# Interleaving the blocks of full and small experts, one by one, in a two-layer diffusion backbone

## The chip, the cores and the metric

The kernel runs on one core of one Trainium2 chip. The metric is the device time in microseconds (us) of one execution of the whole program. Times of single parts come from one profiled execution, read as a page and as a trace.

## What is computed

Two layers of a latent generator over 256 latent and 256 context tokens of width 1024, in float32. Each layer has a mixer (gated linear attention, differential attention, neighbourhood attention) and a channel mixer. The channel mixer of layer 0 is a dense SwiGLU; that of layer 1, which reads only the 256 latent tokens, is a mixture of 8 experts of width 3584, two of them per token:

```python
def swiglu(h, wg, wu, wd):
    return (jax.nn.silu(h @ wg) * (h @ wu)) @ wd

def moe_swiglu(h, w_router, wg, wu, wd):
    t = h.reshape(-1, shp[-1])
    logits = (t @ w_router).astype(jnp.float32)
    top_v, top_i = lax.top_k(logits, TOP_K)
    top_w = jax.nn.softmax(top_v, axis=-1)
    gates = jnp.sum(jax.nn.one_hot(top_i, N_EXPERTS, dtype=jnp.float32) * top_w[..., None], axis=1)
    y = jnp.zeros_like(t)
    for e in range(N_EXPERTS):
        y = y + gates[:, e:e + 1].astype(t.dtype) * swiglu(t, wg[e], wu[e], wd[e])
```

The result is x plus the gated mixture, and one last RMSNorm. The change touches only this expert stage.

## The kernel before

Layer 0 and the mixer of layer 1 fill the first half of the program. Then comes the expert stage, from line 886 on. The kernel routes the tokens, sorts the experts by how many tokens they got (`order_experts`, `order_index`, L988 to L1029), and reads the sorted order into SyncE's registers (`load_order`, L1033), since the weights of expert number e in that order are fetched from an address that the registers give. Expert 0 is taken first whatever its load. The first four are **full** experts with room for 128 tokens, the last four **small** ones with room for 64. Tokens beyond that go through a loop at the end (L1378), which runs only if there are any.

Each expert is worked in 7 **blocks** of 512 of its 3584 inner columns. A block of either kind has three weight matrices, gate, up and down, and each of them comes in two loads of 1 MB (128 partitions x 2048 float32), so a block has 6 loads and an expert 42. All are issued by SyncE's queue in the order of the program.

- A full block (`expert`, L1172): `gate_up` (L1099) for gate and for up, 24 matmuls of 128x512 each, Silu and product (`act_mul`, L1108), transposition and split of the product (`g_T`, L1114), `down` (L1127), 24 matmuls more. Weights are split into a rounded part and a rest, so that three fast matmuls make one precise product: ScalarE writes the rounded part `eh` (L790), VectorE the rest `el` (L791), from the loaded tile `e`. There are three pairs of `eh` and `el`. The down projection of a block follows in the next block, after its gate and up.
- A small block (`expert_small`, L1221): weights are used as they are loaded, in plain float32, with two matmuls of 64 rows side by side: 32 matmuls for gate and up (L1254), 16 for down (L1242).

Loaded tiles live in a ring of named slots of 1 MB (L895 to L904). `first` gives the slots of the first 13 loads; after that the ring turns, and a slot drops out for good at the load number in `until`, when its memory is wanted for something else: ten slots at first, five from load 62 on. A slot is free again when its load has been converted (full) or multiplied (small).

The order of the experts is full 0 to 3, then small 4 to 7, and each expert's last down projection and its scatter into the output (`tail`) are done inside the next expert's first block. Work that is needed once is hooked behind chosen blocks by the table `plan`, whose keys are (expert, block):

```python
plan = {(0, 1): [order_experts], (0, 2): [order_index, lambda: onehots(1, 1, posp)], (0, 4): [lambda: gather_at(1, 1, x01, P), load_order],
        (0, 6): [lambda: row_bc(ga2b, lambda k: modT[1][:, 40 + k, 0:1])],
        (1, 1): [lambda: onehots(2, 2, posp)], (1, 4): [gather_pair],
        (2, 3): [add_x], (2, 5): [stack_ga2],
        (3, 1): [onehots_twice], (3, 4): [gather_rest],
        (4, 3): [lambda: row_bc(gfb, lambda k: gfT[:, k:k + 1])]}
```

`gather_at` brings one expert's tokens together by matmuls (L1078), `gather_pair` those of experts 2 and 3 at once, `gather_rest` those of the four small experts (L1094). PSUM has eight banks: four for gate and up (`pgu`, two tiles of two buffers), two for the down sums (`pdn`), two for everything else (`pmt`).

Of the kernel before, what the change touches and what calls it, by code (L numbers as in the profile page):

```python
# [20 lines left out]
P = 128  # L21
# [68 lines left out]
def hybrid_backbone_kernel(  # L90
# [674 lines left out]
    n_load = [0]  # L765

# [124 lines left out]
    pgu = pool("pgu", 2, space=PSUM)  # L891
# [12 lines left out]
    until = {"xc": 36, "xt": 42, "y": 42, "xh": 62, "xl": 62}  # L904
# [27 lines left out]
    for q in range(2):  # L932
        for t in range(2):
            pt = pgu.tile([P, 512], F32, tag="pg" if t == 0 else "pu", name="pht")
# [128 lines left out]
    def load_e(dram, kk, n):  # L1063
        i = n_load[0]
        n_load[0] += 1
        wh, wl = ready[i] if i in ready else convert(i, slot32(i), dram, kk, n, (mpr, mpr, mpc)[i % 3])
        return wh.rearrange("p (k n) -> p k n", n=n), wl.rearrange("p (k n) -> p k n", n=n)
# [19 lines left out]
    def gather_small():  # L1087
        n = (NE - NBIG) * (P // 2)
        xs = mp.tile([P, KD, n], F32, tag="xeH1", name="xs")
# [18 lines left out]
    def act_mul(pg, pu):  # L1108
        g = mp2.tile([P, 512], F32, tag="eg", name="eg", bufs=2)
        act(g, pg, AF.Silu)  # L1110
        tt(g, g, pu, ALU.mult)
        return g
# [59 lines left out]
    def expert(xe, wg, wu, wd, Sf, gate_col, tail, hooks=None, first=False, end=None):  # L1172
        pds = None
        prev = None
        for j in range(NJ):
# [14 lines left out]
            for f in (hooks or {}).get(j, ()):  # L1190
                f()
# [5 lines left out]
        def t1():  # L1197
            if end:
                tc.keep_in_program_order(nc.scalar.preload_act_table_set(LN_EXP))
                sc = scatter_pre(Sf, gate_col)  # L1200
                new_xg()
                for o in range(2):
                    down_cols(wd, last[0], pds, o)
                    scatter_half(sc, pds, o)
                    end(o)
                return
# [4 lines left out]
        return t0, t1  # L1211

# [8 lines left out]
    def expert_small(xs, wg, wu, wd, e, tail, hooks, end=None):  # L1221
# [4 lines left out]
        def g_Ts(g):  # L1226
# [3 lines left out]
            gt = mp2.tile([P, 4, H], F32, tag="gth", name="gts", bufs=2)  # L1230
# [15 lines left out]
        for j in range(NJ):  # L1246
            ps = pgu.tile([P, 512], F32, tag=("pg", "pu")[j % 2], name="pgs")
# [13 lines left out]
            g = mp2.tile([P, 512], F32, tag="eg", name="eg", bufs=2)  # L1261
# [7 lines left out]
            for f in (hooks or {}).get(j, ()):  # L1269
                f()  # L1270
# [37 lines left out]
    def new_xg():  # L1308
        nonlocal xg
        xg = mp.tile([P, 2, D], F32, tag="xeH0", name="xg")  # L1310
# [31 lines left out]
    def gather_pair():  # L1342
        xes[2] = gather_at(2, 2, xe_tiles(0))

# [3 lines left out]
    def stack_ga2():  # L1348
        for o in range(2):
# [3 lines left out]
    plan = {(0, 1): [order_experts], (0, 2): [order_index, lambda: onehots(1, 1, posp)], (0, 4): [lambda: gather_at(1, 1, x01, P), load_order],  # L1353
            (0, 6): [lambda: row_bc(ga2b, lambda k: modT[1][:, 40 + k, 0:1])],
            (1, 1): [lambda: onehots(2, 2, posp)], (1, 4): [gather_pair],
            (2, 3): [add_x], (2, 5): [stack_ga2],
            (3, 1): [onehots_twice], (3, 4): [gather_rest],
            (4, 3): [lambda: row_bc(gfb, lambda k: gfT[:, k:k + 1])]}
    tail = None
    for e in range(NE):  # L1360
        if e == 0:
            ws = [w[0, 0] for w in (wm_g, wm_u, wm_d)]
        else:
            ws = [w[0, ds(which[e], 1)].rearrange("o a b -> (o a) b") for w in (wm_g, wm_u, wm_d)]
        hooks = {j: f for (ee, j), f in plan.items() if ee == e}
        if e >= NBIG:
            tail = expert_small(xes[NBIG], *ws, e, tail, hooks, square if e == NE - 1 else None)
            continue
        xe, h = (x01, e * P) if e < 2 else (xes[2], (e - 2) * P)
        xv = (xe[0][:, :, h:h + P], xe[1][:, :, h:h + P])  # L1370
        gt_ = gates if e == 0 else gatp
        tail = expert(xv, *ws, lambda t, e=e: S[:, t, e, :], lambda t, e=e, g=gt_: g[:, t, e:e + 1], tail, hooks, e == 0)
    tail[0]()
    tail[1]()
# [3 lines left out]
    with tc.If(cv > 0):  # L1378
# [5 lines left out]
        for blk in range(2):  # L1384
            with tc.For_i(0, NE, 1) as ei:
# [9 lines left out]
                for f in expert(xv, sq_(wm_g), sq_(wm_u), sq_(wm_d), lambda t: S2[:, t, :], lambda t: gc[:, t:t + 1], None):  # L1395
# [36 lines left out]
```

## Time and profile before

| what | value |
|---|---|
| median of 3 runs | 1984.89 us (1984.31 to 1988.7) |
| profiled execution: its own time | 1986.53 us |
| profiled execution: span from first to last instruction | 1984.7 us |
| TensorE (PE) busy | 1836.6 us, 93% |
| VectorE (DVE) busy | 979.5 us, 49% |
| ScalarE (ACT) busy | 758.6 us, 38% |
| bytes read from HBM | 477.48 MB, 241 GB/s over the span |
| mean granted TensorE clock | 0.979 |

The page cuts the span into 40 slices of 49.6 us; slices 21 to 40 are the expert stage. Busy shares are averages over stages with different limits, so each stage has to be looked at by itself. PE matmuls overlap in the pipeline, so a busy PE need not be at its peak, and the length of a matmul's row is longer than the distance from one start to the next.

### The profile page before, as it was taken

How to read it: one execution, taken by the hardware profiler on the slowest of the kernel's cores; microseconds unless marked ns; L12 is line 12 of the kernel's file. 1: busy time of each engine (PE TensorE's matmuls, PEld its weight loads, DVE VectorE, ACT ScalarE, POOL GpSimd, SP SyncE). 2: the span in 40 equal slices, each digit the busy share in tenths (PEclk: the TensorE clock that was granted, in tenths of full speed). 3: DMA queues.
4: the chain of work that ended last, by engine and by line, in shares of the span. 5: the costliest groups of instructions: out<-in, count | busy, mean ns of one | idle time of the engine just before them, and what ended most of it. 6: DMA issues, size and time to landing. Idle time of an engine off the chain costs nothing.

```text
span 1984.7 us, 23236 instructions
## 1 busy us (share of the span) xinstructions
PE 1836.6 (93%) x9168; PEld 1256.5 (63%) x9168; DVE 979.5 (49%) x1296; ACT 758.6 (38%) x967; POOL 45.2 (2%) x73
## 2 busy tenths in 40 slices
PE   7998999999999999899899999999999878787886
PEld 4865766778887878677687878888784222222221
DVE  5474554633333345655678888988984001010101
ACT  4424454422222234245566777767662000000001
POOL 1030000000000000200000000000000000000000
PEclk9999999999999999999989999999999998999998
DMA  9555242342344244543489789999998999999996
GB/s 326 184 168 140 80 137 87 124 131 70 101 131 156 78 127 153 153 129 128 152 294 359 260 295 341 336 355 361 351 343 289 395 390 365 394 381 394 389 389 243
DMA packets 287090, 480.13 MB, mean 242 GB/s; under 512 B 12207, under 2 KB 142637, under 8 KB 286973
## 3 DMA queue, kind: packets, MB, share of 16 engines
q1 hardware_dynamic: 283488, 474.32, 67.8%
q0 software_dynamic: 1232, 2.42, 1.0%
q10 hardware_dynamic: 2252, 1.83, 0.3%
q8 instruction: 74, 1.21, 0.3%
q14 instruction: 44, 0.35, 0.1%
HBM read 477.48 MB, written 1.05 MB: 241 GB/s over the span
## 4 chain that ended last, share of the span: by engine, by line
PE 75%; DMA 14%; DVE 7%; ACT 2%; issue 1%; POOL 0%; SPq 0%; DVEq 0%; ACTq 0%; POOLq 0%
DMA e<-in_w_moe_up_dram 12%; PE pd L1134 8%; PE pgs L1254 7%; PE pds L1242 3%; PE pu L150 3%; PE pg L149 3%; PE pu L151 3%; PE pu L149 3%; PE pg L150 3%; PE pg L151 2%; PE psg L149 2%; PE psg L151 2%; PE psg L150 2%; PE psu L149 2%; PE psu L151 2%; PE psu L150 2%
## 5 line engine op out<-in xcount | busy, mean ns | idle before, releaser
L791 DVE TENSOR_TENSOR el<-e,eh 128x2048 fp32r<-128x2048 f32 (+1 forms) x173 | 375.6, 2190 | 49.2 <-ACT eh L790 48.2
L790 ACT ACTIVATE eh<-e 128x2048 fp32r<-128x2048 f32 (+1 forms) x173 | 316.6, 1839 | 92.7 <-PE pd L1134 31.8
L1254 PE MATMUL pgs<-e,xs 128*64 128x512 f32 x896 | 249.1, 635 | 72.5 <-DMA e<-in_w_moe_up_dram 65.9
L1254 PEld LDWEIGHTS pgs<-e,xs 128*64 128x64 f32 x896 | 70.0, 143 | 237.0 <-DMA e<-in_w_moe_up_dram 107.1
L142 ACT ACTIVATE wh<-w 128x2048 fp32r<-128x2048 f32 (+2 forms) x70 | 125.4, 1791 | 199.5 <-issue 78.3
L143 DVE TENSOR_TENSOR wl<-w,wh 128x2048 fp32r<-128x2048 f32 (+2 forms) x70 | 149.6, 2138 | 96.4 <-ACT wh L142 96.4
L1263 DVE TENSOR_TENSOR eg<-eg,pgs 64x512 f32<-64x512 f32 x28 | 19.3, 690 | 360.1 <-ACT eg L1262 360.1
L1262 ACT ACTIVATE eg<-pgs 64x512 f32<-64x512 f32 x28 | 16.5, 590 | 376.8 <-PE pgs L1254 376.8
L1242 PE MATMUL pds<-e,gts 128*64 128x512 f32 x448 | 126.6, 599 | 0.0
L149 PE MATMUL pg<-eh,xeH 128*128 128x512 f32 x224 | 89.7, 400 | 0.6 <-ACT eh L790 0.6
L149 PE MATMUL psp<-hH,wh 128*128 128x512 f32 (+1 forms) x224 | 86.8, 391 | 3.0 <-ACT hH L274 2.9
L150 PE MATMUL pg<-el,xeH 128*128 128x512 f32 x224 | 89.4, 399 | 0.0
L149 PE MATMUL pu<-eh,xeH 128*128 128x512 f32 x224 | 89.0, 398 | 0.0
L150 PE MATMUL pu<-el,xeH 128*128 128x512 f32 x224 | 88.3, 394 | 0.7 <-DVE el L791 0.6
L149 PE MATMUL psq<-wh,hH 128*128 128x256 f32 x304 | 88.7, 292 | 0.0
L151 PE MATMUL pg<-eh,xeL 128*128 128x512 f32 x224 | 88.5, 395 | 0.0
L151 PE MATMUL psq<-wh,hL 128*128 128x256 f32 x304 | 88.0, 290 | 0.0
L151 PE MATMUL pu<-eh,xeL 128*128 128x512 f32 x224 | 87.7, 392 | 0.0
L150 PE MATMUL psq<-wl,hH 128*128 128x256 f32 x304 | 87.5, 288 | 0.0
L150 PE MATMUL psp<-hL,wh 128*128 128x512 f32 (+1 forms) x224 | 85.6, 382 | 0.0
L151 PE MATMUL psp<-hH,wl 128*128 128x512 f32 (+1 forms) x224 | 85.0, 380 | 0.0
L1134 PE MATMUL pd<-eh,gth 128*128 128x512 f32 x224 | 71.2, 399 | 2.7 <-ACT eh L790 2.5
(504 smaller groups left out, 3445.5 us busy)
## 6 DMA issues: line engine op xcount, KB each, us to landing
e<-in_w_moe_gate_dram SPq DMA_DIRECT2D x111, 1024.0 KB, 7.6
e<-in_w_moe_up_dram SPq DMA_DIRECT2D x111, 1024.0 KB, 7.7
e<-in_w_moe_down_dram SPq DMA_DIRECT2D x111, 1024.0 KB, 7.1
wmod<-in_w_mod_dram SPq DMA_DIRECT2D x96, 512.0 KB, 4.7
w<-in_w_in_dram SPq DMA_DIRECT2D x24, 1024.0 KB, 6.4
w<-in_w_ffn_gate_dram SPq DMA_DIRECT2D x11, 1024.0 KB, 5.7
w<-in_w_ffn_up_dram SPq DMA_DIRECT2D x11, 1024.0 KB, 5.2
w<-in_w_out_dram SPq DMA_DIRECT2D x8, 1024.0 KB, 5.5
```

The source lines that it names most:

```text
L142: act(wh[:, :m], w32[:, :m], AF.Copy)
L143: tt(wl[:, :m], w32[:, :m], f32(wh[:, :m]), ALU.subtract)
L149: mm(ps, lhsT=sh, rhs=mh, start=first, stop=False)
L150: mm(ps, lhsT=sh, rhs=ml, start=False, stop=False)
L151: mm(ps, lhsT=sl, rhs=mh, start=False, stop=last)
L790: act(h3[:, b], w[:, b], AF.Copy)
L791: tt(l3[:, b], w[:, b], f32(h3[:, b]), ALU.subtract)
L1134: mm(pds[o], lhsT=gt[sh][:, q, :], rhs=w[mh][:, k, o * 512:(o + 1) * 512], start=a and j == 0 and q == 0, stop=z and j == NJ - 1 and q == 3)
L1242: mm(pd[0][H * o:H * o + H, :], lhsT=gt[:, q, :], rhs=w[:, k, o * 512:(o + 1) * 512], start=j == 0 and q == 0, stop=j == NJ - 1 and q == 3 ...
L1254: mm(ps[H * o:H * o + H, :], lhsT=xv[:, kk, :], rhs=ws[o][:, k, :], start=kk == 0, stop=kk == KD - 1, skip_group_check=True)
L1262: act(g[0:H], ps[0:H], AF.Silu)
L1263: tt(g[0:H], g[0:H], ps[H:P], ALU.mult)
```

## The change

The two expert functions become generators that stop after each block (`yield`), and a new loop takes one block of the full experts and then one of the small ones, the small ones four blocks behind:

```diff
+    LAG = 4
...
+    def full_ones():
+        tail = None
+        for e in range(NBIG):
+            h = e % 2 * P
+            xv = (x01[0][:, :, h:h + P], x01[1][:, :, h:h + P])
+            gt_ = gates if e == 0 else gatp
+            tail = yield from expert(xv, *weights(e), lambda t, e=e: S[:, t, e, :], lambda t, e=e, g=gt_: g[:, t, e:e + 1], tail, e == 0)
+        tail[0]()
+        tail[1]()
+
+    def small_ones():
+        tail = None
+        for e in range(NBIG, NE):
+            tail = yield from expert_small(xes[NBIG], *weights(e), e, tail, square if e == NE - 1 else None)
+        tail[0]()
+        tail[1]()
+
+    after = {0: [order_experts], 1: [order_index], 2: [onehots_twice], 3: [gather_rest, load_order],
+             4: [lambda: row_bc(ga2b, lambda k: modT[1][:, 40 + k, 0:1]), lambda: onehots(1, 3, posp)],
+             5: [lambda: gather_at(1, 1, x01, P)],
+             8: [add_x], 9: [stack_ga2], 10: [lambda: gather_at(2, 1, x01, 0)], 17: [lambda: gather_at(3, 1, x01, P)],
+             16: [lambda: row_bc(gfb, lambda k: gfT[:, k:k + 1])]}
+    bigs, smalls = full_ones(), small_ones()
+    for i in range(NBIG * NJ + LAG):
+        next(bigs, None)
+        if i >= LAG:
+            next(smalls, None)
+        for f in after.get(i, ()):
+            f()
+    next(smalls, None)
     finish()
```

Blocks 0 to 3 of the full experts stand alone, then come 24 pairs of a full and a small block, then the last 4 small blocks alone. The hooks move with it: the small experts' tokens are gathered after full block 3, the order is read into the registers there too, and experts 2 and 3 are gathered one by one (blocks 10 and 17) into the places that experts 0 and 1 leave free, where they were gathered together.

Memory is shared out anew, so that both kinds can be open at once: gate and up get one PSUM bank each instead of two, the small experts one for gate and up and one for down; the products have one buffer per kind; the small experts' tokens take the slot `xh` and the output the other half. The ring keeps `xl` for good, and the drop-outs come earlier:

```diff
-    pgu = pool("pgu", 2, space=PSUM)
+    pgu = pool("pgu", 1, space=PSUM)
...
-    until = {"xc": 36, "xt": 42, "y": 42, "xh": 62, "xl": 62}
+    until = {"xc": 26, "xt": 42, "y": 42, "xh": 22}
...
-        wh, wl = ready[i] if i in ready else convert(i, slot32(i), dram, kk, n, (mpr, mpr, mpc)[i % 3])
+        n_conv[0] += 1
+        wh, wl = ready[i] if i in ready else convert(i, slot32(i), dram, kk, n, (mpr, mpr, mpc)[(n_conv[0] - 1) % 3])
...
-        g = mp2.tile([P, 512], F32, tag="eg", name="eg", bufs=2)
+        g = mp2.tile([P, 512], F32, tag="eg", name="eg")
...
-            ps = pgu.tile([P, 512], F32, tag=("pg", "pu")[j % 2], name="pgs")
+            ps = pgu.tile([P, 512], F32, tag="ps", name="pgs")
...
-                pd[0] = pdn.tile([P, 512], F32, tag=f"pd{e % 2}", name="pds")
+                pd[0] = pdn.tile([P, 512], F32, tag="pds", name="pds")
```

Lines of the changed kernel stand 1 or 2 below those of before (L784, the load of a full expert, becomes L785; L790 and L791 become L791 and L792).

Three places show how the instructions move. The first is **SyncE's queue**. Before, in the middle of the small experts, every load is one of a small block (`e32` is the ring's tile), and waits for PE to have freed the slot:

```order
L1218 DMA e32_12251<-in_w_moe_gate_dram 128x4x512 [waits DMAHW2_49,PE_49]
L1218 DMA e32_12253<-in_w_moe_up_dram 128x4x512 [waits DMAHW3_49,PE_49]
L1218 DMA e32_12270<-in_w_moe_gate_dram 128x4x512 [waits DMAHW4_49,PE_49]
L1218 DMA e32_12272<-in_w_moe_up_dram 128x4x512 [waits DMAHW5_49,PE_49]
L1218 DMA e32_12285<-in_w_moe_down_dram 128x2x1024 [waits DMAHW6_49,PE_49]
L1218 DMA e32_12291<-in_w_moe_down_dram 128x2x1024 [waits DMAHW7_49,PE_49]
```

In the changed kernel six loads of a full block (L785) and six of a small one (L1218) take turns:

```order
L785 DMA e32_9114<-in_w_moe_gate_dram 128x4x512 [waits DMAHW2_49,PE_49]
L785 DMA e32_9132<-in_w_moe_gate_dram 128x4x512 [waits DMAHW3_49,PE_49]
L785 DMA e32_9160<-in_w_moe_up_dram 128x4x512 [waits DMAHW4_49,PE_49]
L785 DMA e32_9178<-in_w_moe_up_dram 128x4x512 [waits DMAHW5_49,PE_49]
L785 DMA e32_9199<-in_w_moe_down_dram 128x2x1024 [waits DMAHW6_49,PE_49]
L785 DMA e32_9217<-in_w_moe_down_dram 128x2x1024 [waits DMAHW7_49,PE_49]
L1218 DMA e32_9268<-in_w_moe_gate_dram 128x4x512 [waits DMAHW0_49,DVE_49]
L1218 DMA e32_9270<-in_w_moe_up_dram 128x4x512 [waits DMAHW1_49,DVE_49]
L1218 DMA e32_9287<-in_w_moe_gate_dram 128x4x512 [waits DMAHW2_49,DVE_49]
L1218 DMA e32_9289<-in_w_moe_up_dram 128x4x512 [waits DMAHW3_49,DVE_49]
L1218 DMA e32_9302<-in_w_moe_down_dram 128x2x1024 [waits DMAHW4_49,DVE_49]
L1218 DMA e32_9308<-in_w_moe_down_dram 128x2x1024 [waits DMAHW5_49,DVE_49]
```

With six slots and six loads per block, a full load now waits for PE to have used the small load in its slot, and a small one for VectorE to have converted the full load.

The second place is **ScalarE**, in the middle of the full experts. Before, conversions (`eh`) of the next loads stand close behind one another, with only the Silu (`eg`) and the split of the transposed product (`gth`) between them:

```order
L790 ACTIVATE eh_9105<-e32_9104 128x2048 [waits DMAHW1_49,DVE_49,PE_49]
L790 ACTIVATE eh_9123<-e32_9122 128x2048 [waits DMAHW2_49,DVE_49,PE_49]
L790 ACTIVATE eh_9151<-e32_9150 128x2048 [waits DMAHW3_49,DVE_49,PE_49]
L790 ACTIVATE eh_9169<-e32_9168 128x2048 [waits DMAHW4_49,DVE_49,PE_49]
L1161 ACTIVATE yHL_9080<-xT_70 128x512 [waits DVE_49] x2
L1110 ACTIVATE eg_9186<-pg_9103 128x512 [waits PE_49]
L790 ACTIVATE eh_9192<-e32_9191 128x2048 [waits DMAHW5_49,Activation_49]
```

In the changed kernel the small block's Silu (`es`) and the copy of its transposed product (`gts`) stand ahead of the next full block's first conversion:

```order
L791 ACTIVATE eh_10193<-e32_10192 128x2048 [waits DMAHW1_49,DVE_49,PE_49]
L1123 ACTIVATE gth_10300<-pgt_10295 128x512 [waits PE_49]
L1262 ACTIVATE es_10242<-pgs_10210 64x512 [waits PE_49]
L287 ACTIVATE gts_10398<-pgt_10393 128x256 [waits PE_49]
L791 ACTIVATE eh_10260<-e32_10259 128x2048 [waits DMAHW0_49,DVE_49]
L791 ACTIVATE eh_10278<-e32_10277 128x2048 [waits DMAHW1_49,DVE_49]
L791 ACTIVATE eh_10306<-e32_10305 128x2048 [waits DMAHW2_49,DVE_49]
L791 ACTIVATE eh_10324<-e32_10323 128x2048 [waits DMAHW3_49,DVE_49,PE_49]
L1112 ACTIVATE eg_10341<-pg_10258 128x512 [waits PE_49]
```

The third place is **PE** at the same spot, the end of a small block and the start of the next full one. `pds` is the small expert's down sum, `pgt` the transposed product, `pg` the full expert's gate:

```order
L1242 MATMUL pds_10245<-e32_10246,gts_10228 64x512 [waits DMAHW6_49]
L1242 MATMUL pds_10245<-e32_10246,gts_10228 64x512 x3
L1229 MATMUL pgt_10393<-ident_58,es_10242 128x64 [waits DVE_49]
L1229 MATMUL pgt_10393<-ident_58,es_10242 128x64 x3
L1242 MATMUL pds_10245<-e32_10252,gts_10228 64x512 [waits DMAHW7_49]
L1242 MATMUL pds_10245<-e32_10252,gts_10228 64x512 x3
L149 MATMUL pg_10258<-eh_10260,xeH_7918 128x512 [waits Activation_49]
L150 MATMUL pg_10258<-el_10261,xeH_7918 128x512 [waits DVE_49]
```

Before, the same down matmuls were followed by the next small block's gate and up, which wait for loads alone:

```order
L1242 MATMUL pds_11873<-e32_11880,gts_11856 64x512 [waits DMAHW4_49]
L1242 MATMUL pds_11873<-e32_11880,gts_11856 64x512 x3
L1254 MATMUL pgs_11886<-e32_11887,xs_11448 64x512 [waits DMAHW5_49]
L1254 MATMUL pgs_11886<-e32_11889,xs_11448 64x512 [waits DMAHW6_49]
L1254 MATMUL pgs_11886<-e32_11887,xs_11448 64x512
```

So PE now goes from a small block straight into a full one, whose first matmul waits for ScalarE and whose second waits for VectorE.

## Rows read from the trace of the kernel before

**Rows 1.** The page, span and slices (busy tenths, GB/s per slice of 49.6 us).
```profile
span 1984.7 us, 23236 instructions
DMA  9555242342344244543489789999998999999996
GB/s 326 184 168 140 80 137 87 124 131 70 101 131 156 78 127 153 153 129 128 152 294 359 260 295 341 336 355 361 351 343 289 395 390 365 394 381 394 389 389 243
```

**Rows 2.** Windows (us: busy of PE, PEld, DVE, ACT, POOL, PEclk, DMA share, GB/s).
```profile
1062.00:1090.00 28.00, 26.63 (x132) 21.75 (x131) 22.79 (x17) 17.28 (x15) 0.00 (x0) 1.00 1.05 389
1300.00:1500.00 200.00, 199.40 (x910) 161.32 (x908) 173.52 (x107) 137.80 (x92) 0.00 (x0) 1.00 0.98 351
1000.00:1526.00 526.00, 519.49 (x2344) 414.86 (x2345) 437.73 (x305) 354.71 (x247) 0.00 (x0) 0.99 0.91 328
1550.00:1900.00 350.00, 286.64 (x1176) 92.91 (x1174) 32.06 (x55) 17.79 (x34) 0.00 (x0) 0.97 1.03 386
```

**Rows 3.** Chain of waits, full experts: start us, us, what (down of two blocks).
```profile
1172.37 5.55 PE pd L1134 x24
1189.42 5.55 PE pd L1134 x24
```

**Rows 4.** Chain of waits, small experts, one block.
```profile
1579.29 3.22 PE pgs L1254 x13
1584.68 10.53 DMA e<-in_w_moe_up_dram
1595.26 3.22 PE pgs L1254 x13
```

**Rows 5.** SyncE's waits, 1000 to 1500, then 1540 to 1960 (total us, times, longest).
```profile
SPq L784 <- DVE el L791: 367.7, 139, 15.4
SPq L1035 <- DVE cnti L1029: 0.3, 1, 0.3
...
SPq L1218 <- PE pgs L1254: 228.7, 94, 7.5
```

**Rows 6.** Loads: count on the page; SyncE's timeline; queue, 962 to 1083.
```profile
e<-in_w_moe_gate_dram SPq DMA_DIRECT2D x111, 1024.0 KB, 7.6
...
909.97 7.93 SPq L784 DMA_DIRECT2D e<-in_w_moe_gate_dram  x2
917.94 0.51 SPq L784 DMA_DIRECT2D e<-in_w_moe_up_dram  x1
...
q1 hardware_dynamic: 17752, 36.66, 83.8%
```

**Rows 7.** Groups by line (xcount, busy, mean ns) and timeline (start, us): single steps.
```profile
L791 DVE TENSOR_TENSOR el<-e,eh 128x2048 fp32r<-128x2048 f32 x24 | 54.9, 2290 | 8.8 <-ACT eh L790 8.5
L790 ACT ACTIVATE eh<-e 128x2048 fp32r<-128x2048 f32 x24 | 46.1, 1920 | 15.6 <-PE pd L1134 8.4 <-PE pg L151 3.8 <-PE pu L151 3.4
L1263 DVE TENSOR_TENSOR eg<-eg,pgs 64x512 f32<-64x512 f32 x22 | 15.2, 690 | 290.7 <-ACT eg L1262 290.7
L1262 ACT ACTIVATE eg<-pgs 64x512 f32<-64x512 f32 x22 | 13.0, 590 | 308.2 <-PE pgs L1254 308.2
L289 DVE COPY gts<-pgt 128x256 f32<-128x256 f32 x11 | 4.7, 424 | 15.9 <-PE pgt L1229 15.9
...
1584.58 0.46 PE L1229 MATMUL pgt<-ident,eg 64*128 64x64 f32 x4
1962.63 5.37 PE L1242 MATMUL pds<-e,gts 128*64 128x512 f32 x24
```

**Rows 8.** Chain of waits: full blocks around a gather; gather of the small experts.
```profile
1075.47 5.56 PE pd L1134 x24
1098.40 5.55 PE pd L1134 x24
...
1466.80 1.08 PE pga L1094 x9
```

**Rows 9.** SyncE's timeline at the end: last weight loads, output.
```profile
1945.54 13.90 SPq L1218 DMA_DIRECT2D e<-in_w_moe_down_dram  x4
1976.31 2.19 SPq L1333 DMA_DIRECT2D out_dram<-xg  x2
```

More of the change, by code (lines that the diff above doesn't have):

```diff
@@ L765, in hybrid_backbone_kernel @@
     n_load = [0]
+    n_conv = [0]
     def open_ring():
@@ L933, in hybrid_backbone_kernel @@
         for t in range(2):
-            pt = pgu.tile([P, 512], F32, tag="pg" if t == 0 else "pu", name="pht")
+            pt = (pgu if q == 0 else pdn).tile([P, 512], F32, tag=(("pg", "pu"), ("pd0", "pd1"))[q][t], name="pht")
             for k in range(4):
@@ L1088, in gather_small @@
         n = (NE - NBIG) * (P // 2)
-        xs = mp.tile([P, KD, n], F32, tag="xeH1", name="xs")
+        xs = mp.tile([P, KD, n], F32, tag="xeH0", name="xs")
         for m in range(0, KD, 2):
@@ L1170, in scatter_half, with expert @@
                 tt(xtk[:, t, cs], xtk[:, t, cs], py, ALU.add)
-    def expert(xe, wg, wu, wd, Sf, gate_col, tail, hooks=None, first=False, end=None):
+    def expert(xe, wg, wu, wd, Sf, gate_col, tail, first=False):
         pds = None
@@ L1189, in expert @@
             prev = g
-            for f in (hooks or {}).get(j, ()):
-                f()
+            yield
         last = []
@@ L1197, in t1 @@
         def t1():
[L1198 to L1206, printed above, removed]
             down(wd, last[0], NJ - 1, pds)
@@ L1211, in expert, with run_expert @@
         return t0, t1
+    def run_expert(*args):
+        g = expert(*args)
+        while True:
+            try:
+                next(g)
+            except StopIteration as stop:
+                return stop.value
     def load_raw(dram, kk, n):
@@ L1219, in load_raw, with expert_small @@
         return wv
-    def expert_small(xs, wg, wu, wd, e, tail, hooks, end=None):
+    def expert_small(xs, wg, wu, wd, e, tail, end=None):
         H = P // 2
@@ L1229, in g_Ts @@
                 nc.tensor.transpose(pt[:, q * H:(q + 1) * H], g[0:H, q * P:(q + 1) * P], ident[0:H, 0:H])
-            gt = mp2.tile([P, 4, H], F32, tag="gth", name="gts", bufs=2)
+            gt = mp2.tile([P, 4, H], F32, tag="gts", name="gts")
             copy_bal(gt, pt[:, 0:4 * H].rearrange("p (q n) -> p q n", n=H))
@@ L1260, in expert_small @@
                         tail[0]()
-            g = mp2.tile([P, 512], F32, tag="eg", name="eg", bufs=2)
+            g = mp2.tile([P, 512], F32, tag="es", name="es")
             act(g[0:H], ps[0:H], AF.Silu)
@@ L1268, in expert_small @@
             prev = g
-            for f in (hooks or {}).get(j, ()):
-                f()
+            yield
         last = []
@@ L1309, in new_xg @@
         nonlocal xg
-        xg = mp.tile([P, 2, D], F32, tag="xeH0", name="xg")
+        xg = mp.tile([P, 2, D], F32, tag="xeH1", name="xg")
     ssq4 = mp.tile([P, 2, 2], F32, name="ssq4")
@@ L1340, in hybrid_backbone_kernel @@
     gather_at(0, 1, x01)
-    def gather_pair():
-        xes[2] = gather_at(2, 2, xe_tiles(0))
     def gather_rest():
@@ L1351, in stack_ga2 @@
             nc.vector.tensor_copy(ga2s[hs], part(ga2b, o)[hs])
[L1353 to L1358, printed above, removed]
@@ L1359, in hybrid_backbone_kernel @@
-    tail = None
-    for e in range(NE):
-        if e == 0:
[L1362 to L1372, printed above, removed]
@@ L1373, in hybrid_backbone_kernel, with weights @@
-    tail[0]()
-    tail[1]()
+    LAG = 4
+    def weights(e):
+        if e == 0:
+            return [w[0, 0] for w in (wm_g, wm_u, wm_d)]
+        return [w[0, ds(which[e], 1)].rearrange("o a b -> (o a) b") for w in (wm_g, wm_u, wm_d)]
+    def full_ones():
[7 more added lines that the diff above has]
+        tail[1]()
@@ L1394, in hybrid_backbone_kernel @@
                 sq_ = lambda w: w[0, ds(ei, 1)].rearrange("o a b -> (o a) b")
-                for f in expert(xv, sq_(wm_g), sq_(wm_u), sq_(wm_d), lambda t: S2[:, t, :], lambda t: gc[:, t:t + 1], None):
+                for f in run_expert(xv, sq_(wm_g), sq_(wm_u), sq_(wm_d), lambda t: S2[:, t, :], lambda t: gc[:, t:t + 1], None):
                     f()
```

## Prediction

> **What bounds the kernel now.** I read the slices first. In the expert stage the DMA engines look full almost everywhere, yet the bytes moved per slice differ: around 350 GB/s or less in slices 21 to 31, around 390 from slice 32 on [rows 1]. So two stages with different limits hide behind one row of nines, and I read windows of each.
>
> In the full experts (1300 to 1500 us) PE is busy 199.4 of 200 us and the loads come at 351 GB/s. In the small ones (1550 to 1900) PE is busy 286.6 of 350 us, VectorE 32, ScalarE 18, and the loads come at 386 GB/s [rows 2]. The chain of waits says the same in time. Full blocks follow each other every 1189.42 - 1172.37 = 17.05 us, and the chain runs through PE matmuls all the way [rows 3]. Small blocks follow every 1595.26 - 1579.29 = 15.97 us, of which 10.53 us are a wait for a load [rows 4]. SyncE's own waits close the picture: in the full stage its queue stood 367.7 us waiting for VectorE to free a slot [rows 5], so the loads wait for the engines there. In the small stage SyncE waits too (228.7 us for PE's matmuls), but PE itself waits for the loads that are under way: 386 GB/s is the rate at which the loads come when they set the pace.
>
> The full experts are thus bound by PE with DMA time to spare, the small ones by DMA with PE time to spare. The change lays one beside the other.
>
> **The change part by part.** One load is 1.0486 MB; at 386 GB/s it takes 2.716 us. One pair of blocks has 12 loads, 32.6 us of DMA. A small block costs PE 48 matmuls: 24 of them took 5.37 us when nothing was missing, 0.224 each, so 10.7 us, and 0.46 us of transposes [rows 7], 11.2 in all. With the full block's 17.05 that is 28.25 us of PE per pair. Before, the two took 17.05 + 15.97 = 33.0 us, so a pair alone saves little. The gain is elsewhere: the 526 us from 1000 to 1526 hold 28 x 17.05 = 477 us of full blocks and 49 us of other PE work and stalls, at only 328 GB/s on average [rows 2]. This time, too, can now lie under loads.
>
> *The sum, by DMA.* There are 8 x 42 = 336 loads (111 of each matrix plus three into the ring's split slot [rows 6]). The fifth full block's turn ends PE's down at 1075.47 + 5.56 = 1081 us [rows 8]; up to there the order is the old one, but for the gather of the small experts, 32 matmuls which came nine in 1.08 us [rows 8], 4 us. So the first small block starts at 1085. By 1083 the queue had moved 36.66 MB since 962, 35 loads, and three had been issued before (two gate, one up) [rows 6]: 38. The new ring loses two slots by then, so I take 37, and 299 are left. 299 x 2.716 = 812 us. The end: SyncE's last issue was at 1945.54 + 13.90 = 1959.4 [rows 9], and PE ran the last 24 matmuls until 1968.0 [rows 7], the last 8 of them, 1.8 us, on the last load. It landed after 1959.4 and before 1966.2; I take 1964, nearest to the middle, and so 1984.7 - 1964 = 21 us of ending, which the change leaves as it is. 1085 + 812 + 21 = 1918.
>
> *What PE adds.* At the turn from small to full, ScalarE and VectorE stand in the way: ScalarE's queue holds the small block's Silu and copy ahead of the next conversion. Silu 0.59 and product 0.69 lie under half of the down matmuls (8 x 0.224 = 1.79); after the transposes come copy 0.42, rounded part 1.92, rest 2.29 [rows 7], 4.63 us, of which the other 1.79 us of down and the first matmul (0.23) are cover: PE idles 2.6 us. Bounds: nothing where PE would have waited for the load anyway, 4.63 if the cover fails too. I take 2.6, since the cover stands in PE's order. PE then needs 28.25 + 2.6 = 30.85 of the 32.6 us, 1.75 to spare. Converting early helps little while loads set the pace, because the load lands last.
>
> *Gathers.* One gather in a full block cost 1098.40 - 1075.47 - 17.05 = 5.9 us [rows 8]. Three of them (experts 1, 2, 3; the last two were one) fall into pairs with 1.75 us to spare, so each may cost 4.2: 12.6 us. Bounds: nothing if loads already in the ring bridge it, 18 if none do. I take 12.6, as the ring has only six slots. The adding of x, the two broadcasts and the scatters are shorter and spread over other pairs; they take what is spare there.
>
> *Costed at nothing.* The single PSUM banks and product buffers: the next user of `pg` comes after a whole other block, and in the four full blocks alone after 24 down matmuls (5.55 us [rows 3]) against a Silu of about 0.6 [rows 7]; uncovered, each would be that Silu, under 3 us in all. The register loads: SyncE passes them one block sooner; it waited 0.3 us there [rows 5] and has loads out ahead. The ring's six slots instead of five at the end: nothing, or a gain, as below. Alternating PSUM groups, `n_conv`, generators: no instruction of weight.
>
> *Total.* 1918 + 12.6 = 1930.6 of span. The profiled execution's own time is 1986.53 - 1984.7 = 1.8 above its span, and 1.6 above the median of 1984.89. So I predict **1931 us**, 2.7% less. At 389 GB/s, the best long stretch amid full blocks [rows 2], without gather loss, it would be 1085 + 299 x 2.696 + 21 = 1912; I take 1910 as the low end.
>
> **The rivals.**
>
> *PE and its helpers become the bound.* For it: PE's part is nearly as long. After 1085 come 23 full blocks (392 us), the last down (5.6), 24 small ones (269), 24 turns (62), the 49 us of other work and about 6 for the split gather, then four small blocks alone (64) and the ending: 1085 + 848 + 21 = 1954. Against: part of the 49 us are stalls of the old order, and every wait for a load hides some. It decides when the turn costs more than the 4.35 us between 28.25 and 32.6. With 4.63 instead of 2.6 in all 24 pairs it would be 1954 + 49 = 2003, slower. I place it at 1945 to 1980.
>
> *The loads' ceiling is lower beside conversions: slower.* The DMA share reads 0.98 at 351 GB/s in the full stage and 1.03 at 386 in the small one [rows 2]. If those 0.98 mean full, the two streams on ScalarE and VectorE hold back the queue, and laying conversions beside small blocks brings the slow rate everywhere: 1.0486 MB at 351 GB/s is 2.99 us, 299 of them 893, and 1085 + 893 + 21 + 12.6 = 2012 us, 1.3% slower. It decides at 2.90 us per load, 362 GB/s, where the gain is gone. Against it stand 28 us at 389 GB/s in the middle of the full experts, with PE, VectorE and ScalarE at work [rows 2], and SyncE's 367.7 us of waiting for slots [rows 5], which explain 351 without a ceiling; so I give it little. The Trainium skill ("DMA: Bandwidth & Descriptors", section Bandwidth) has a rule on this side: it gives about 358 GB/s as what the HBM allows one core and says that this binds between HBM and SBUF; that would be 2.93 us a load and 1994 us, no gain. The trace does not agree: by that rule the small stage could not hold 386 GB/s for 350 us.
>
> *Better than the sum.* The loads run at 390 and more with a deeper ring, and gathers vanish under them: below 1910.
>
> *It does not do what it says.* The queue orders show the blocks alternating on SyncE, ScalarE and PE, so I give this nothing.
>
> **How the numbers follow.** Forecast, DMA-bound throughout, 1910 to 1945: 0.66. PE-bound: 0.22, of which 0.18 up to 1980 and 0.04 at or above today's time. Lower ceiling: 0.08, about half of it still faster or equal. Better than the sum: 0.04. A measurement of this kernel can tell about 0.2% (4 us) from no change. Faster by more: 0.66 + 0.18 + 0.04 and 0.03 of the ceiling's 0.08, 0.91. Within it: 0.02 of the PE case and 0.01 of the ceiling, 0.03. Slower: 0.02 and 0.04, 0.06. The range 1910 to 1965 holds the forecast, two thirds of the PE case (0.12) and the mild part of the ceiling (0.02).
>
> **What would show it.** Right: windows of the 24 pairs at 380 GB/s or more; a full block's down every 32 to 33 us; PE's longest waits on loads or on conversions that wait for loads; 2.6 us or less of idle PE between a small block's last down matmul and the next `el`; the first small block near 1085, the last weight load near 1910. Wrong: pairs of 34 us and more with PE waiting for ScalarE or VectorE while loads have landed (first rival); pairs of 34 us and more with SyncE never waiting for a slot and the loads near 355 GB/s (second); a first small block much later than 1085, which would mean that the register loads or the gather stall the queue.

## The result and the profile after

| what | before | changed |
|---|---|---|
| median, runs side by side | 1984.68 us (1984.31 to 1988.7, 4 runs) | 2010.94 us (2009.51 to 2013.9, 4 runs) |
| ratio to before, 95% interval | 1 | 1.013 [1.0112, 1.0147] |
| span of the profiled execution | 1984.7 us | 2008.2 us |
| mean granted TensorE clock | 0.979 | 0.965 |

The change made the kernel 1.3% slower; 1931 us, 2.7% faster, had been predicted, and the time lies 46 us above the range. The page of the changed kernel (span; clock granted to TensorE, DMA share in tenths and GB/s, per slice of 50 us) answers to [rows 1]:

```profile
span 2008.2 us, 23245 instructions
PEclk9998999999999999999899998999989999999998
DMA  9554242332443244533578899989999999999996
GB/s 324 186 167 131 89 139 73 126 126 69 121 145 120 86 134 152 148 118 118 210 269 303 328 334 335 335 327 357 359 345 337 342 368 368 380 357 355 365 358 258
```

The two rates of [rows 1] have become one in between, 337 to 380 GB/s in slices 28 to 39, and the clock row reads 8 in some slices of the stage. Windows of the 24 pairs (busy us and count of PE, PEld, DVE, ACT, POOL, then granted clock, DMA share, GB/s), beside [rows 2]:

```profile
1300.00:1500.00 200.00, 183.10 (x754) 104.74 (x752) 91.47 (x70) 72.67 (x56) 0.00 (x0) 0.95 0.94 345
1088.00:1908.00 820.00, 759.08 (x3158) 455.07 (x3156) 394.76 (x286) 308.41 (x239) 0.00 (x0) 0.94 0.94 348
```

PE was busy 199.4 of 200 us in the full stage before at a clock of 1.00 [rows 2]; now it is busy 183 of 200 at 0.95. So PE waits and runs slower, while the loads come at 348 GB/s in place of 386. The chain of waits (start us, us, what) shows one turn from a small block to a full one:

```profile
1236.95 1.72 PE pds L1242 x7
1238.67 0.39 PE pgt L1229 x4
1239.06 1.89 PE pds L1242 x8
1240.97 0.02 ACT gts L287
1241.25 1.91 ACT eh L791
1243.18 2.30 DVE el L792
1245.53 0.80 PE pg L150
```

The small block's product is transposed (`pgt`) by 1239.06, but its copy `gts` starts only at 1240.97, when the second half of the preceding down product (`pds`) has ended; behind the copy ScalarE writes `eh`, and VectorE `el`. From 1240.95 to 1245.53, 4.58 us, the chain holds no PE (beside it PE runs one gate matmul, 0.49 us). The waits from 1100 to 1900 us (us in total, times, longest) name the same releaser, and under it SyncE's own, which answer to [rows 5]:

```profile
ACT gts L287 <- PE pds L1242: 26.8, 8, 4.1
DVE gts L289 <- PE pds L1242: 17.6, 7, 3.8
...
SPq L1218 <- DVE el L792: 345.3, 127, 7.1
SPq L785 <- PE pgs L1254: 192.9, 79, 7.2
```

The reason is in the memory share-out: before, `gts` used a tag with two buffers (L1230); in the change it has a tag of its own with one. The down matmuls read that buffer to the end. The copies alternate between ScalarE and VectorE. Where VectorE does it, `eh` has no copy ahead of it and runs early, and the turn is shorter. This is another turn in the same chain, 1572.65 to 1575.35:

```profile
1570.76 1.89 PE pds L1242 x8
1572.67 0.04 DVE gts L289
1573.02 2.29 DVE el L792
1575.35 0.59 PE pg L150
```

Between 1160 and 1890 us the chain has 20 such gaps without a load's landing in them, from 2.70 to 4.80 us, 77 us together, 3.9 each. What follows a gap is seen in windows of 2 us around the first turn:

```profile
1232.00:1234.00 2.00, 2.00 (x12) 0.76 (x10) 0.00 (x0) 0.59 (x1) 0.00 (x0) 1.00 0.45 80
...
1242.00:1244.00 2.00, 0.49 (x1) 0.19 (x1) 0.82 (x1) 2.00 (x2) 0.00 (x0) 1.00 1.04 400
1244.00:1246.00 2.00, 0.47 (x1) 0.47 (x2) 2.00 (x2) 2.00 (x2) 0.00 (x0) 0.63 1.06 413
1246.00:1248.00 2.00, 2.00 (x6) 1.52 (x6) 2.00 (x2) 0.75 (x1) 0.00 (x0) 0.50 1.02 410
...
1252.00:1254.00 2.00, 2.00 (x10) 1.65 (x9) 1.43 (x1) 0.73 (x2) 0.00 (x0) 1.00 1.05 388
```

After the gap PE works at 0.50, the lower of its two levels, until about 1251 (the window 1250 to 1252 reads 0.66), and gets 6 matmuls into 2 us in place of 10. The last column speaks against a lower ceiling: loads run at 385 to 413 GB/s from 1242 to 1254, with ScalarE and VectorE converting. They fall behind elsewhere: at 1232, before the turn, they drop to 80 GB/s, and SyncE's waits say for what, a slot that is still to be converted or multiplied.

### The profile page after: what moved, and what is told of

The parts are those of the page before. It is cut to its first block, busy times and chain, and to the rows that moved or that the text cites. A ratio compares the mean times of both kernels' runs of the same rounds, so it can differ in the third digit from the quotient of the medians.

```text
span 2008.2 us, 23245 instructions
## 1 busy us (share of the span) xinstructions
PE 1874.6 (93%) x9200; PEld 1276.8 (64%) x9200; DVE 982.1 (49%) x1299; ACT 757.3 (38%) x971; POOL 45.2 (2%) x73
## 3 DMA queue, kind: packets, MB, share of 16 engines
q0 software_dynamic: 1232, 2.42, 0.9%
## 4 chain that ended last, share of the span: by engine, by line
PE 81%; DVE 8%; DMA 5%; ACT 3%; issue 1%; SPq 0%; POOL 0%; ACTq 0%; DVEq 0%; POOLq 0%
PE pgs L1254 10%; PE pd L1136 8%; PE pds L1242 4%; PE pg L150 4%; PE pg L151 3%; PE pg L149 3%; DVE el L792 3%; PE pu L150 3%; PE pu L149 3%; PE pu L151 3%; DMA e<-in_w_moe_up_dram 2%; PE psg L149 2%; PE psu L151 2%; PE psu L150 2%; PE psu L149 2%; PE psg L151 2%
## 5 line engine op out<-in xcount | busy, mean ns | idle before, releaser
L792 DVE TENSOR_TENSOR el<-e,eh 128x2048 fp32r<-128x2048 f32 (+1 forms) x174 | 377.6, 2190 | 118.8 <-ACT eh L791 118.3
L791 ACT ACTIVATE eh<-e 128x2048 fp32r<-128x2048 f32 (+1 forms) x174 | 316.2, 1833 | 117.1 <-PE pg L151 74.9
L1254 PE MATMUL pgs<-e,xs 128*64 128x512 f32 x896 | 233.9, 605 | 7.1 <-DMA e<-in_w_moe_up_dram 6.4
L1254 PEld LDWEIGHTS pgs<-e,xs 128*64 128x64 f32 x896 | 64.3, 137 | 132.0 <-issue 119.9
L150 PE MATMUL pg<-el,xeH 128*128 128x512 f32 x224 | 107.7, 481 | 35.6 <-DVE el L792 35.6
L149 PE MATMUL pg<-eh,xeH 128*128 128x512 f32 x224 | 104.6, 467 | 18.4 <-ACT eh L791 18.4
L151 PE MATMUL pg<-eh,xeL 128*128 128x512 f32 x224 | 101.9, 455 | 0.0
L1263 DVE TENSOR_TENSOR es<-es,pgs 64x512 f32<-64x512 f32 x28 | 19.3, 690 | 154.2 <-ACT es L1262 154.2
L1123 ACT ACTIVATE gth<-pgt 128x512 fp32r<-128x512 f32 x28 | 16.6, 592 | 194.1 <-PE pgt L1119 194.1
L150 PEld LDWEIGHTS pg<-el,xeH 128*128 128x128 f32 x224 | 51.7, 231 | 54.2 <-DVE el L792 43.0
```

Of the source, the lines that this page charges most:

```text
L149: mm(ps, lhsT=sh, rhs=mh, start=first, stop=False)
L150: mm(ps, lhsT=sh, rhs=ml, start=False, stop=False)
L151: mm(ps, lhsT=sl, rhs=mh, start=False, stop=last)
L791: act(h3[:, b], w[:, b], AF.Copy)
L792: tt(l3[:, b], w[:, b], f32(h3[:, b]), ALU.subtract)
L1123: act(gh, pv, AF.Copy)
```

## The experiments

Three theories stood at the start. **1, the turn:** PE idles about 4.5 us from a small block to a full one, and what runs after it at the half clock adds to that. **2:** loads are slower beside conversions (the second rival of the prediction). **3:** the new shares of memory cost the time, not the order. Every ratio is to the kernel before, which ran beside each group; its median was 1984.68 us beside the change and 1988.23 to 1989.94 beside the others, so differences in us between rows of the table are good to about 5 us.

| run | median us | ratio, 95% interval | 1100 to 1900 us: clock, GB/s |
|---|---|---|---|
| the change | 2010.94 | 1.0130 [1.0112, 1.0147] | 0.94, 350 |
| a_lag28: new shares, old order | 1993.32 | 1.0021 [1.0005, 1.0037] | |
| d_cold2: transposes between the down halves | 2003.82 | 1.0091 [1.0072, 1.011] | |
| d_warm2: and 16 dummy matmuls a turn | 2043.79 | 1.0293 [1.0276, 1.0311] | |
| c2_early: gate loads and conversions ahead | 1949.38 | 0.9811 [0.9777, 0.9845] | 0.98, 373 |
| b_gts2: second buffer of `gts` | 1969.63 | 0.9908 [0.9883, 0.9933] | 0.98, 367 |
| d_cold3: both transposes early | 1981.01 | 0.9963 [0.9948, 0.9978] | 0.96, 363 |
| d_warm3: and 16 dummies a turn | 1998.14 | 1.0040 [1.0025, 1.0054] | 0.99, 355 |
| d_warm8: 8 dummies | 1987.11 | 0.9988 [0.9969, 1.0007] | 0.98, 361 |
| f_early_gts2: c2_early and b_gts2 | 1948.83 | 0.9807 [0.9779, 0.9835] | 0.99, 376 |
| e_two: two full, two small in turn | 1957.98 | 0.9851 [0.9811, 0.989] | 0.97, 372 |
| g_two_gts2: e_two and b_gts2 | 1959.82 | 0.9856 [0.984, 0.9873] | 0.98, 371 |
| g_two_early: and gate loads ahead | 1941.76 | 0.9766 [0.975, 0.9782] | 0.99, 380 |

**The shares of memory alone (a_lag28).**

```diff
-    LAG = 4
+    LAG = NBIG * NJ
```

> The changed kernel with its new shares of memory (single PSUM banks, one product buffer per kind, ring of six), but all 28 full blocks first and the small ones after them, as before: only one turn from full to small is left. Theory 1, the turn: each of 24 turns from a small to a full block costs an idle PE of about 4.5 us and then some microseconds at half clock; without turns the time is that of before, 1980 to 1992 us. Theory 2, loads are slower beside conversions: here they are not beside small blocks, so also 1980 to 1992. Theory 3, the new shares of memory cost the time: it stays at 2005 to 2015.

Measured: 1993.32 us, 0.2% above before, just clear of no change, and 1 us above the span that was expected. Theory 3 falls as it was put: the single PSUM banks, the single products and the smaller ring cost about 4 us while the order is the old one. One of these shares is the single buffer of `gts`, and in the small stage of this run (1500 to 1900 us) its copies wait for `pds` too, 10 times on ScalarE, 35.9 us, and 9 times on VectorE, 22.8 us. It costs next to nothing there, where no conversion stands behind the copy and PE waits for loads. So a share of memory that does no harm in the old order may still do it in the new one. A window of its small stage also shows what loads do when they set the pace: 394 GB/s.

```profile
1700.00:1900.00 200.00, 165.24 (x678) 53.42 (x680) 18.45 (x32) 9.38 (x18) 0.00 (x0) 0.97 1.04 394
```

**The turn taken away (c2_early).** From the sixth full block on, the two gate loads of a full block are issued and converted ahead of the small block that precedes it; its first matmul is kept behind that block.

```diff
-            w = load_e(w_ap[half * 512:(half + 1) * 512, j * 512:(j + 1) * 512].rearrange("(k p) n -> p k n", p=P), 4, 512)
+            w = pre[half] if pre else load_gu(w_ap, j, half)
...
+            if nxt:
+                pre = nxt(j + 1)
             yield
```

> The changed kernel with the two gate loads of the next full block issued and converted ahead of the small block's loads, and the first gate matmul kept behind the small block: the turn finds converted weights. Theory 1: no idle at the turn, loads set the pace at 32 to 33 us per pair: 1925 to 1945 us, 380 GB/s or more in the pairs. Theory 2: loads stay near 355 GB/s, pairs at 35 us, 2000 to 2015. Theory 3: above 2000 as well.

Measured: 1949.38 us, faster than both kernels, 62 us less than the change, and 4 us above theory 1's span. Its chain at a turn:

```profile
1462.52 1.87 PE pds L1251 x8
1464.38 0.43 PE pg L150
1464.82 0.24 PE pg L153
```

PE goes from `pds` straight into `pg`, and from the second one on the matmuls are 0.24 us apart. Its windows settle theory 2:

```profile
1300.00:1500.00 200.00, 194.40 (x839) 115.67 (x838) 105.60 (x77) 82.11 (x62) 0.00 (x0) 0.98 1.02 380
1500.00:1700.00 200.00, 190.72 (x829) 113.19 (x828) 105.52 (x79) 83.61 (x64) 0.00 (x0) 0.99 1.02 384
```

With more conversions in the same 200 us than the change (VectorE 106 against 91 us), the loads come at 380 and 384 GB/s. The ceiling of 351 GB/s that theory 2 needs is not there. Over 1100 to 1900 us the mean is 373, not the 380 expected. The Trainium skill ("DMA: Bandwidth & Descriptors", section Bandwidth) gives about 358 GB/s as the limit of one core and, in a note of the same section, as each core's share when both cores of a domain stream. These windows, of a program on one core, lie above it.

**The buffer given back (b_gts2).** One edit to the change, and one that pays for it in memory:

```diff
-        gl = mp2.tile([P, 4, P], F32R, tag="gtl", name="gtl", bufs=2)
+        gl = mp2.tile([P, 4, P], F32R, tag="gtl", name="gtl")
...
-            gt = mp2.tile([P, 4, H], F32, tag="gts", name="gts")
+            gt = mp2.tile([P, 4, H], F32, tag="gts", name="gts", bufs=2)
```

> The small block's transposed product gets its second buffer back (the full block's gives one up for it). Theory 1 (the turn): the idle from the last down matmul of a small block to the first gate matmul of the next full one falls from about 4.5 us to the two conversions' 4.2 less what of them now runs beside the down matmuls, about 2.6 us; over 24 turns up to 24 x 1.9 = 46 us, so 1955 to 1990 us, and loads above 355 GB/s from 1100 to 1900 us. Theory 2 (loads slower beside conversions): 2011 us within 4, loads at 350 GB/s as before. Theory 3 (new shares of memory) fell with the run that had the new shares alone.

Measured: 1969.63 us, 41 us less than the change and within theory 1's bounds. No copy waits for `pds` any longer; from 1100 to 1900 us all waits of `gts` are for its own transposes:

```profile
ACT gts L287 <- PE pgt L1229: 30.3, 12, 10.3
DVE gts L289 <- PE pgt L1229: 14.0, 10, 7.4
```

and the chain at a turn now goes around the second half of the down product:

```profile
1431.95 1.87 PE pds L1242 x8
1433.82 0.40 PE pgt L1229 x4
1434.52 1.91 ACT eh L791
1436.45 2.30 DVE el L792
1438.80 0.71 PE pg L150
```

From `pgt` to `pg` it is still 4.58 us, but the other 8 `pds` matmuls, 1.9 us, run beside it. PE's own idle is 2.7 us, which is the 2.6 of the prediction. So the cover failed for want of one buffer, and that alone was worth half of what separates the change from its forecast.

The 41 us are more than the shorter idle gives. The gate matmuls have three lines on a page. This is one of them (count | busy us, mean ns | idle just before, us), first of the change, then of b_gts2:

```profile
L150 PE MATMUL pg<-el,xeH 128*128 128x512 f32 x224 | 107.7, 481 | 35.6 <-DVE el L792 35.6
L150 PE MATMUL pg<-el,xeH 128*128 128x512 f32 x224 | 98.4, 439 | 29.0 <-DVE el L792 28.9
```

All three lines together are busy 314.2 us in the change and 289.4 in b_gts2 (267.6 before), while the up matmuls, further from the turn, stay at 264. PE's whole busy time falls by the same 24.8 us, 1874.6 to 1849.8, for the same 9200 matmuls. The spans differ by 43.6 us: 24.8 of them are gate matmuls, the first ones behind a turn, that take less time at a higher mean clock (0.979 against 0.965), and 18.8 are less idle PE.

**Both (f_early_gts2).** The edits of c2_early and b_gts2 together.

> The next full block's two gate loads and their conversions ahead of the small block (the run that took 1949 us), and the second buffer of the small block's transposed product with it. Theory 1: with the turn's conversions already ahead, the second buffer takes away what is left of waiting behind the transposed copy at the start of a small block: 1925 to 1949 us. Theory 2: no change, 1949 us within 4.

Measured: 1948.83 us against 1949.38. The upper end of theory 1's span, but no gain: once the gate conversions stand ahead, nobody waits for that copy where it matters. Beside b_gts2 it is 21 us less, so with the buffer in place the early conversions are worth 21 us, not 62: the two remedies take away much of the same wait. Its loads ran at 388 GB/s from 1700 to 1900 us.

**Half the turns (e_two).**

```diff
-        if i >= LAG:
+        if i >= LAG and i % 2:
+            next(smalls, None)
             next(smalls, None)
```

> The change itself, but two full blocks and then two small ones in turn: 12 turns from a small to a full block in place of 24, all else as in the change. Theory 1 (the turn): the cost per turn is (2011 - 1949) / 24 = 2.6 us, so 12 turns fewer save about 31 us, 1970 to 1990 us. Theory 2 (loads slower beside conversions): the same work in the same stretch, 2011 us within 6. If instead a turn's cost comes from the six load slots running empty or full in longer runs of one kind: above 2011 us.

Measured: 1957.98 us, 53 us below the change, more than theory 1 had expected: 4.4 us for each turn that is gone, not 2.6. I had priced a turn by what c2_early saved over 24 turns; but in that run the loads set part of the pace (380 GB/s), so it need not show a turn's whole price. Theory 2 is refuted a second time, since the work beside the loads is the same.

**Half the turns and the buffer (g_two_gts2).** The edits of e_two and b_gts2 together.

> Two full blocks and two small ones in turn (the run of 1958 us), with the second buffer of the small block's transposed product. Theory 1: each of the 12 turns that are left idles 2.7 us instead of 4.6, and small blocks that follow one another no longer wait for one another's product: up to 12 x 1.9 = 23 us less, 1935 to 1950 us, and no less than the 1931 us at which loads at 386 GB/s bind. Theory 2: 1958 us within 4. A second buffer that was worth 41 us with 24 turns must be worth at most half with 12.

Measured: 1959.82 us, no less than without it: a miss. The chain at a turn says why:

```profile
1263.90 0.02 ACT es L1262
1264.40 1.91 ACT eh L791
1266.33 2.30 DVE el L792
1268.67 0.50 PE pg L150
```

With two small blocks in a row the second one's Silu (`es`), not the copy, stands last ahead of `eh`; in other turns it is the landing of the full block's gate load. By this chain, the buffer helps only where its copy is the last thing that ScalarE is held up by.

**And the gate loads ahead (g_two_early).** The edits of c2_early with them, for every second full block:

```diff
-                if n < EARLY or n >= NBIG * NJ:
+                if n < EARLY or n >= NBIG * NJ or n % 2:
```

> Two full blocks and two small ones in turn, the second buffer, and at each of the 12 turns the next full block's two gate loads and conversions ahead of the small blocks. Theory 1: what PE idles at the turns is gone, loads bind at 380 to 386 GB/s from 1100 to 1900 us, 1928 to 1945 us. If the loads that stand ready early hold two of the six slots over two small blocks and starve these, it is slower than without them.

Measured: 1941.76 us, ratio 0.9766 [0.975, 0.9782], the fastest of all and 2.3% faster than before. Its loads:

```profile
1100.00:1900.00 800.00, 759.62 (x3332) 447.33 (x3330) 396.05 (x299) 310.68 (x243) 0.00 (x0) 0.99 1.01 380
```

At 380 GB/s over the whole stretch it is within 11 us of the 1931 that the sum by DMA gave with 386.

**What the half clock costs by itself (d_cold2, d_warm2, d_cold3, d_warm3, d_warm8).** The idea: fill the idle of the turn with matmuls that nothing reads, so that the clock stays up, and compare with the same kernel without them. The first pair put the small product's transposes between the two halves of `down_s`:

```diff
+                if hf == 0 and mid is not None:
+                    mid.append(g_Ts(mid[0]))
...
+                for _ in range(WARM):
+                    tc.keep_in_program_order(mm(pd_, lhsT=htH[:, 0, 0:P], rhs=htH[:, 0, 0:512], start=True, stop=True))
```

> The changed kernel with the transposition of a small block's product written where the scheduler had put it anyway, between the two halves of its down projection. Control for the next run. All theories: 2003 to 2018 us, with the granted clock at 0.5 for some microseconds after each turn.

> The same, with 16 matmuls of 128x512 on old data into a PSUM tile that nobody reads, between a small block's last down matmul and the next full block's first: 3.7 us of work in the gap of about 4.5 us. Theory 1 with the clock as second half of the cost: the wait stays, but the matmuls behind it run at full clock, so about 24 x 2.6 = 62 us less than the control, 1945 to 1965, granted clock of the stage near 1.0. Theory 1 without the clock (the idle gap is all): within 10 us of the control. Theory 2: within 10 us of the control.

Measured: 2003.82 and 2043.79 us. The control itself is 0.4% below the change, so its edit was not quite neutral. The pair is no test of the clock, as the chain of the second shows:

```profile
1389.92 3.86 PE pwarm L1184 x16
1394.01 0.45 PE pgt L1121 x4
1394.98 1.92 ACT eh L793
```

The dummies (`pwarm`) stood ahead of the full block's transposes (`pgt`, L1121), ScalarE's copy of these stood ahead of `eh`, and so the dummies came on top of the conversions instead of beside them. In the next three runs the full product is transposed before the small block begins, so that the dummies stand alone:

```diff
-            if prev is not None:
-                gt = g_T(prev)
-            elif tail:
+            if prev is None and tail:
...
+            gt = g_T(g)
```

They differ in `WARM`: 0, 16 and 8.

> The product of a full block is transposed before the small block begins, and the small block's own product between the two halves of the preceding small down product; no dummy work. Control for the next run. Theory 1: the wait behind the transposed copies moves but the idle before the first gate matmul stays between 2 and 4.6 us, 1970 to 2015 us. Theory 2: 2011 us within 6.

> As the run before it, with 16 dummy matmuls of 128x512 (3.4 to 3.9 us at full clock) into a PSUM tile that nothing reads, alone between the last down matmul of the small block and the first gate matmul of the full one, where TensorE is otherwise idle. It leaves nothing of the result out. If the half clock after the idle is a cost of its own: the granted clock stays at 1.00 after each turn and the first gate matmuls take about 392 ns instead of 467 to 481, 24 turns x up to 2.6 us = up to 60 us less than the run before. If the half clock costs nothing on the path (the loads set the pace meanwhile): within 10 us of the run before. Theory 2: the same as the run before within 6 us.

> As the control of 1981 us (both transposes early), with 8 dummy matmuls of 128x512 in place of 16 at each of 23 turns: 1.9 us at full clock, less than the shortest idle there (2.7 us), so that they take the place of idle only. If the half clock after the long turns (pg matmuls 445 to 472 ns against 390) costs time of its own: 23 turns x 12 x 70 ns x 0.5 to 1 = 10 to 20 us less than the control, 1960 to 1972 us. If it costs nothing on the path: 1981 us within 5. The 16 dummies cost 17 us since at 3.86 us they outlast the short turns by 1.2 us; 8 must not cost that by either account.

Measured: 1981.01, 1998.14 and 1987.11 us. The clock did what was intended. At a turn with 4.59 us of gap, the control first, then with 8 dummies:

```profile
1445.00:1447.00 2.00, 1.14 (x3) 0.95 (x4) 2.00 (x2) 2.00 (x2) 0.00 (x0) 0.62 1.02 410
1447.00:1449.00 2.00, 2.00 (x7) 1.56 (x6) 2.00 (x2) 0.08 (x1) 0.00 (x0) 0.53 1.01 399
```

```profile
1451.00:1453.00 2.00, 0.76 (x3) 0.67 (x4) 2.00 (x2) 2.00 (x2) 0.00 (x0) 1.00 1.03 411
1453.00:1455.00 2.00, 2.00 (x10) 1.64 (x10) 2.00 (x2) 0.46 (x1) 0.00 (x0) 1.00 1.04 408
```

But the time did not fall: +17 us with 16 dummies, +6 with 8 (here the intervals of the two ratios overlap). Neither account of the expectations had that. PE's rows show where the time went. The gate matmuls did get shorter, from 302.4 us busy in the control to 281.2 with 8 and 273.9 with 16 dummies, and PE's waits just ahead of them fell from 55.1 to 25.7 and 6.0 us. But the dummies themselves were busy 53.6 and 93.1 us. That makes 53.6 - 21.2 - 29.4 = +3.0 us and 93.1 - 28.5 - 49.1 = +15.5 us, near what was measured. So the half clock did cost PE time, some 28 us of gate matmuls in the control, and the dummies took more than they gave back. No run raised the clock and did nothing else, so what the clock alone would bring on the whole time stays open.

That the control is itself 30 us faster than the change was not taken apart. Its page shows where: the small blocks' matmuls (`pgs` and `pds`) are busy 327.1 us in place of 357.7. Why is not shown.

## Why the prediction was wrong

- **The start was right.** PE's first small matmuls began at 1087.82 us, predicted 1085. Here is PE's timeline (start us, us):

```profile
1087.82 4.51 PE L1254 MATMUL pgs<-e,xs 128*64 128x512 f32 x20
```

- **The loads' ceiling was right.** The second rival, 2012 us, names nearly the time that came out, by accident, and is false all the same: loads run at 380 to 388 GB/s beside conversions as soon as slots come free in time (c2_early, f_early_gts2). A time that fits is no evidence for its mechanism; the windows are.
- **The step that failed is "What PE adds".** The text took 2.6 us of idle per turn "since the cover stands in PE's order", with 4.63 "if the cover fails too" as the other bound. The cover did stand in PE's order, but the copy beside which it should have lain could not start. The chain's gaps were 3.9 us on average, 4.6 in the longer kind; with the buffer given back, 41 us of the 80 between 1931 and 2011 were gone. The same slip stands in "Costed at nothing": it looked at each single buffer for who uses it next in the full blocks (`pg`, the product) and missed `gts`, whose last reader, the second half of the small down product, ends just before the turn. The order listings already showed it: `pds` reads `gts_10228` on both sides of the transposes into `pgt_10393`.
- **A term was missing.** The clock was taken as 1.00 as in the full stage before. It read 0.94 from 1088 to 1908: of a pair of blocks that is 0.06 x 36 = 2.1 us of PE's full speed. PE's rows have nearly the same: the gate matmuls were busy 314.2 us against 267.6 before, 46.6 us more, 2.0 for each of the 23 turns into a full block.
- **The pairs.** Full downs, 17.05 us apart when alone [rows 3], follow each other from 1222.45 to 1901.37 in 19 steps, 35.73 us a pair; 32.6 were forecast, and 12.6 us of gathers for all pairs together. From the first small block (1087.89) to the last one beside a full block (1908.12) it is 820 us in 23 steps, where the forecast has 23 x 32.6 + 12.6 = 762.4. So 58 of the 78 us by which the span, 2008.2, exceeds the forecast's 1930.6 lie in the pairs. PE's side by the prediction's own terms: 28.25, 3.9 for the turn, 2.0 for the 49 us of other work over 24 pairs, which the text left to the 1.75 us to spare, and 2.0 for the clock: 36.2, a little above the 35.73 measured. Turn and other work alone make 34.2, already past the loads' 32.6.
- **The first rival happened.** It said that PE decides when a turn costs more than 4.35 us, and 2003 us with the cover gone everywhere. It got 0.04 for times at or above today's. That was the error of judgement: 1.75 us of margin per pair, over 24 pairs, hung on a bound which had not been held against the one buffer that sets it.
- **"Converting early helps little while loads set the pace, because the load lands last" fell too.** Its condition did not hold, since PE set the pace. Converting early saved 62 us on the change, 21 with the buffer in place, and 18 from g_two_gts2 to g_two_early. The load that is early is the one that needs 4.2 us of conversion after it lands; the small block's loads, which need none, can come last.
- **The end** looks as the text had it, four small blocks that wait for loads as in [rows 4], with waits of 10.12, 12.26 and 12.29 us in the chain. It is longer than the sum by DMA left for it: from 1908.12 to the end 100 us, where the forecast has 1930.6 - 1085 - 762.4 = 83. PE's terms in the first rival fit (a small block 11.2, the last down 5.6, four small blocks 64, the ending 21: 102). These 17 us, and 3 at the start, are the rest of the 78.

## What to carry to other kernels

Where two kinds of work alternate on a shared engine, each change of kind is a place where a queue in order must be walked through by hand: list what stands ahead of the first instruction that PE waits for, and for each of these the last reader of the buffer that it writes, since a cover in PE's order is worth nothing if the work under it cannot start. Give a second buffer to what is copied just before such a turn, or put the load with the longest way to its first matmul ahead of the other kind's block, and turn less often: here each of these alone made 2011 us into 1970, 1949 and 1958, and the last two together, with the buffer, into 1942. Their gains do not add up, since they remove much of the same wait. Matmuls put into the idle to hold the clock up took more time than they gave back. When the margin per step is small against the uncertainty of one term in it, the chance of the other sign is not small.

## What the runs showed of the hardware

TensorE's granted clock was 1.00 before the 4.58 us gap that ended at 1245.53, read 0.63 in the window in which the gap ended and 0.50 in the next, and was back at 1.00 at 1252, after about 6 us of dense work; and this in a kernel where PE is busy 93% of the time. A gap of 2.70 us was seen with both outcomes: 0.50 afterwards at 1576 in the change, and in the control d_cold3, after a gap that ended at 1478.02, no fall:

```profile
1477.00:1479.00 2.00, 0.98 (x4) 0.85 (x5) 2.00 (x2) 1.20 (x2) 0.00 (x0) 1.00 1.05 387
1479.00:1481.00 2.00, 2.00 (x10) 1.62 (x10) 1.66 (x2) 1.49 (x1) 0.00 (x0) 1.00 1.06 398
```

The Trainium skill ("TensorE: Matmul & The Clock Gate", section "HAM oscillation — how this bites in real kernels") describes the same pattern, a matmul kernel that waits once in every step and starts each step slow. The rows agree on it: the gate matmuls behind the turns were busy 314.2 us in the change against 267.6 before. That holding the clock up makes the whole kernel faster no run showed.
